# SBUF pools that wait per tile, output blocks with their own part tiles, and layer-1 modulation in parts over the whole FFN

## The chip, the cores and the metric

The kernel runs on one core of one Trainium2 chip. The metric is the device time of one execution in microseconds (us), median of several runs. Engines are named as in the profile: PE is TensorE (PEld its weight loads), DVE is VectorE, ACT is ScalarE, POOL is GpSimd, SP is SyncE, whose queue issues every DMA.

## The reference

Two blocks in a row. The first block has two layers over 512 tokens: stream 0 is the 256 context tokens, stream 1 the 256 latent tokens, D = 1024. A conditioning vector per stream gives, for each layer, six modulation rows of 1024 (shift, scale and gate of the mixer, the same of the FFN):

```
mods = silu(c) @ mod_w[l] + mod_b[l]          # rows 0..5
x = x + row2 * mixer(rmsnorm(x) * (1 + row1) + row0)
x = x + row5 * conv_ffn(rmsnorm(x) * (1 + row4) + row3)
```

Layer 0's mixer is gated linear attention and an mLSTM side by side, their outputs concatenated and multiplied by `even_w_out`; layer 1's is a state-space scan. `conv_ffn` is up-projection (1024 to 2 x 2816), a depthwise 3 x 3 convolution, silu gate, down-projection (2816 to 1024). In layer 1 only stream 1's output is needed past the mixer. The second block is one hybrid attention layer over the 256 latent tokens.

## The kernel before, in words

All activations lie features-first: 128 partitions by (8 feature chunks, 512 tokens). Each float32 weight block is loaded into a tile `st` (1 MB, 2048 columns), rounded to float16 `whi` on ACT, and the rest `st - whi` is written as bfloat16 `wlo` on DVE, or on POOL where `eng=self.G` is given (`get_w`, L318). A product takes three bfloat16/float16 passes: hi by hi, hi by lo, lo by hi (`proj_fm`, L328). `st` comes from `wst` (three buffers), the parts from `wsp` (three), unless a call names other pools (`pool`, `parts`).

Modulation row `r` of layer `l` is computed by `mod_steps` (L495), a generator of four steps per row. Each step loads 1 MB of `mod_w`. A *whole* step multiplies float32 by float32 (`cs`, 8 matmuls of 256 columns); a step *in parts* first splits the weights and multiplies by `c3`, the vector in three bfloat16 terms side by side (16 matmuls). One PSUM tile gathers the four steps, then ACT and two small matmuls make the row. `mod_first` does rows 0 and 1 of layer 0 at the start.

The stages around the change:

- `layer0_mixer` (L540): gated linear attention, then the mLSTM over four heads (`close`, L914, normalizes and writes a finished head). Their pools `gp`, `ev`, `mp` close. `xT`, the residual stream, is loaded. The tail: `whole_c` (L487) builds `cs` anew, rows 2, 3 and 4 follow as whole steps, then the four blocks of `even_o`. Blocks 0 and 1 read the attention half of the mixer's output (`h[0..3]`), blocks 2 and 3 the mLSTM half. Block 0 runs over all 512 tokens; blocks 1 to 3 per stream. `add_residual` (L533) adds the gated result to `xT`. After stream 0 comes its norm (`norm_stream`, L529).
- `ffn(0)` (L971): stream 1's norm, with two blocks of up weights begun on stream 0. 22 up blocks follow, each with convolution (`conv`, L990: ACT, then 18 DVE operations), gate (ACT, POOL) and split. After each of the first 16 blocks one modulation step is taken, after each later one two: row 5 of layer 0 and rows 0 and 1 of layer 1 in parts, rows 2 to 5 of layer 1 whole, from the pool `mp` with one buffer. Then eight down blocks of two halves (`down`, L1038), the last two per stream, with layer 1's norm of stream 0 between.
- `layer1_mixer` (L1067), `ffn(1)`, `block2` (L1421).

The order within each engine's queue is made ahead of time by Tile's scheduler (`schedule_with_timeline_sim`, L1918): among the instructions that are ready in a simulated timeline, the first in program order goes next. A later stage's work can thus come long before its place in the program, if its tiles and buffers are free; on the chip each queue then runs in that order.

A pool opened on bytes of closed pools waits: by default (`"pool"`) every tile of it waits for all users of all those closed pools; with `reuse_waits="tile"` each tile waits only for the users of the earlier tiles on its own bytes. Before, PSUM pools and the weight pools `wst`, `wsp`, `stage`, `nx`, `fw` have the latter; the others have the default.

Of the kernel before, what the change touches and what calls it, by code (L numbers as in the profile page):

```python
# [10 lines left out]
F32 = mybir.dt.float32  # L11
# [5 lines left out]
ALU = mybir.AluOpType  # L17
# [216 lines left out]
BOTH = ((0, 0, 256), (1, 256, 512))  # L234
# [14 lines left out]
class Program:  # L249
# [14 lines left out]
    def pool(self, name, bufs=1, space=None, stack=None, **kw):  # L264
        if space is not None:
            kw["space"], kw["reuse_waits"] = space, "tile"
        return (stack or self.ctx).enter_context(self.tc.tile_pool(name=name, bufs=bufs, **kw))

    def weight_sets(self, n):

        if self.w_stack is not None:
            self.w_stack.close()
        self.w_stack = self.ctx.enter_context(ExitStack())
        self.wst, self.wsp = [self.pool(t, n, None, self.w_stack, side="right", reuse_waits="tile") for t in ("wst", "wsp")]

# [127 lines left out]
    def start(self, c0):  # L403
# [9 lines left out]
        cv = ep("cv").rearrange("p (k s) -> p k s", s=2)  # L413
        self.cs = c0.tile([128, 8, 32], F32, name="cs")
        self.G.memset(self.cs, 0.0)
# [70 lines left out]

    def whole_c(self, pool):  # L487

        self.cs = pool.tile([128, 8, 32], F32, name="cs")
        self.G.memset(self.cs, 0.0)  # L490
        cs = self.cs[:, :, 0:2]
        self.tt(cs, self.c3[:, :, 2:4], self.c3[:, :, 4:6], ALU.add)
        self.tt(cs, cs, self.c3[:, :, 0:2], ALU.add)

    def mod_steps(self, l, r, tag="mm", eng=None, pool=None, parts=None, whole=False):  # L495
# [44 lines left out]
    def layer0_mixer(self):  # L540
        h, I = self.h, self.I
# [20 lines left out]
        with ExitStack() as tail:  # L562
            self.whole_c(self.pool("c0", 1, None, tail))
            for r in (2, 3, 4):
                for _ in self.mod_steps(0, r, whole=True):
                    pass
            w = self.get_w(I["even_o"][0], 4, 512)
            for c in range(4):
                ps = self.mm("eo")
                self.proj_fm(ps, w, c * 128, 128, h, 0, 512, nk=4)  # L570
                self.add_residual(ps, 0, 2, c, BOTH)

            w = [self.get_w(I["even_o"][b], 4, 512) for b in range(1, 4)]
            for s in range(2):
                for b in range(1, 4):
                    for c2 in range(2):
                        ps = self.mm("eo")
                        for c in range(2):
                            self.proj_fm(ps[:, c * 256:c * 256 + 256], w[b - 1], (2 * c2 + c) * 128, 128, h,
                                         256 * s, 256 * s + 256, nk=4, h0=4 * (b // 2))  # L580
                        for c in range(2):
                            self.add_residual(ps[:, c * 256:], 0, 2, 4 * (b % 2) + 2 * c2 + c, ((s, 0, 256),), 256 * s)
                if s == 0:
                    self.norm_stream(0, 1, 0, "ml")
        self.dbg("xmid0", self.xT)

# [384 lines left out]
    def ffn(self, l, streams):  # L971
# [6 lines left out]
        if both:  # L978

            self.norm_stream(l, 1, 1)  # L980
            first = []
            for i in range(2):
                w = self.get_w(I["w_up"][l, i], 8, 256, self.G)
                first.append((w, [self.mm("up") for _ in range(2)]))
                for c in range(2):
                    self.proj_fm(first[i][1][c][:, :256], w, c * 128, 128, h, 0, 256)
# [18 lines left out]
        with ExitStack() as ph:  # L1005
            fp = self.pool("fp", 1, None, ph)
            f2 = self.pool("f2", 3, None, ph)
            stage = self.pool("stage", 1 if both else 3, None, ph, reuse_waits="tile")
            fcw = fp.tile([128, 44, 9], F32, name="fcw")
            self.nc.sync.dma_start(fcw, I["fcw"][l].rearrange("p (c j) -> p c j", c=44))  # L1010
            hid = self.pair(fp, "hid", [128, 22, n])
            if both:
                mp = self.pool("mp", 1, None, ph)
                self.whole_c(mp)
                mods = chain(chain.from_iterable(self.mod_steps(*m, eng=self.G, pool=mp, parts=mp) for m in ((0, 5), (1, 0), (1, 1))),
                             chain.from_iterable(self.mod_steps(1, r, pool=mp, whole=True) for r in (2, 3, 4, 5)))
            for i in range(22):
                begun = both and i < 2
                if begun:
# [14 lines left out]
                self.split(hid[0][:, i], hid[1][:, i], sg[:, :n], eng=self.G)  # L1034
                for _ in range(l == 0 and (1 if i < 16 else 2)):
                    next(mods, None)

# [11 lines left out]
            for k in range(6 if both else 8):  # L1049
                self.add_residual(down(k, [weights(k, j) for j in range(2)], 0, n), l, 5, k, streams, t0)  # L1050
                if not both:
                    self.before_norm(k)
# [339 lines left out]
    def ahead(self):  # L1392

        self.nx_stack = self.ctx.enter_context(ExitStack())
        self.nx = self.pool("nx", 6, None, self.nx_stack, side="right", reuse_waits="tile")
        self.first_mg = []
# [24 lines left out]
    def block2(self):  # L1421
# [19 lines left out]
        self.weight_sets(2)  # L1441
        fw = self.pool("fw", 2, None, self.w_stack, side="right", reuse_waits="tile")

# [499 lines left out]
```

## Time and profile before

| | us |
|---|---|
| three runs | 1723.3, 1730.93, 1726.06 |
| median | 1726.06 |
| the profiled execution | 1721.83 |
| its span, first to last instruction | 1720.0 |
| granted TensorE clock over the span | 0.959 of full speed |

Busy time is the time in which an engine's instructions run. In the rows, "idle before" is the time that the engine stood still ahead of an instruction, and behind it stands what ended that. Instructions of a helper such as `tt` (L294), `stt` (L303), `act` (L306) or `proj_fm` (L332) all have the helper's line, so tile names tell them apart. Granted clock 1.0 is 2.4 GHz, half of it 1.2.

### The profile page before, as it was taken

The numbers are of one execution on the slowest core, as the hardware profiler recorded it, in microseconds if no ns is written. First come the engines' busy times: TensorE is split into PE (matmuls) and PEld (weight loads), VectorE is DVE, ScalarE is ACT, GpSimd is POOL, SyncE is SP. The second block draws the span as 40 slices with busy tenths as digits, with TensorE's granted clock in tenths as the row PEclk, the third lists the DMA queues.
The fourth block names the chain that finished last, engine by engine and source line by source line (L and its number), as shares of the span: only waits on it lengthen the run. The fifth ranks groups of instructions, "written<-read, shape, count | busy, mean of one in ns | idle before, by whom it ended". The sixth has DMA issues, their size and how long they took to land.

```text
span 1720.0 us, 31609 instructions
## 1 busy us (share of the span) xinstructions
PE 1592.1 (93%) x12912; PEld 1094.0 (64%) x12978; DVE 1190.9 (69%) x2604; ACT 824.0 (48%) x1354; POOL 489.6 (28%) x267
## 2 busy tenths in 40 slices
PE   6999999869999979999889898879999999999998
PEld 3566865556444434476556565658887787777877
DVE  5888746688777753346876767779987796366734
ACT  4746524336554422224653635446656454466542
POOL 0000000036997521001100101039964321342150
PEclk8999999889999979999999898989999999999999
DMA  9222127423555544232322222236446253243551
GB/s 378 97 83 75 52 91 272 158 98 109 187 196 189 178 172 138 94 97 86 109 74 98 74 99 74 99 128 217 170 152 219 104 188 123 92 167 129 219 174 50
DMA packets 37730, 236.77 MB, mean 138 GB/s; under 512 B 4304, under 2 KB 5072, under 8 KB 14672
## 3 DMA queue, kind: packets, MB, share of 16 engines
q1 hardware_dynamic: 37584, 234.74, 38.9%
q8 instruction: 102, 1.67, 0.4%
q14 instruction: 44, 0.36, 0.1%
HBM read 233.68 MB, written 1.05 MB: 136 GB/s over the span
## 4 chain that ended last, share of the span: by engine, by line
PE 75%; DVE 11%; issue 4%; ACT 3%; DMA 3%; POOL 2%; SPq 0%; ACTq 0%; DVEq 0%; POOLq 0%
PE up L332 17%; PE dn L332 8%; PE sx L332 5%; PE fm L332 4%; PE mg L332 3%; PE sz L332 3%; PE br L332 2%; PE so L332 2%; PE mod L509 2%; DVE wlo L294 2%; ACT whi L306 2%; POOL wlo L294 2%; PE mqk L332 2%; PE eo L332 2%; PE tm L339 1%
## 5 line engine op out<-in xcount | busy, mean ns | idle before, releaser
L332 PEld LDWEIGHTS <-whi 128*128 128x128 f16 (+2 forms) x5240 | 515.8, 100 | 266.0 <-issue 45.9
L294 POOL TENSOR_TENSOR wlo<-st,whi 128x2048 bf16<-128x2048 f32 (+2 forms) x102 | 358.6, 3520 | 648.2 <-ACT whi L306 597.9
L306 ACT ACTIVATE whi<-st 128x2048 f16<-128x2048 f32 (+3 forms) x206 | 343.5, 1673 | 303.8 <-issue 49.8
L303 DVE SCALAR_TENSOR_TENSOR u<-up,fcw,u 128x189 f32<-128x189 f32 (+3 forms) x792 | 303.7, 432 | 71.9 <-ACT u L306 61.1
L332 PEld LDWEIGHTS <-wlo 128*128 128x128 bf16 (+2 forms) x2620 | 260.7, 100 | 129.8 <-issue 14.5
L294 DVE TENSOR_TENSOR wlo<-st,whi 128x2048 bf16<-128x2048 f32 (+3 forms) x104 | 223.6, 2152 | 103.0 <-ACT whi L306 102.0
L332 PE MATMUL up<-hh,whi 128*128 128x256 f16 (+1 forms) x736 | 237.2, 325 | 2.1 <-ACT hh L306 1.8
L332 PE MATMUL up<-hh,wlo 128*128 128x256 f16 (+1 forms) x736 | 236.3, 323 | 1.9 <-issue 0.8
L332 PE MATMUL up<-hl,whi 128*128 128x256 bf16 (+1 forms) x710 | 225.9, 320 | 2.7 <-DVE hl L303 2.7
L332 PE MATMUL dn<-hidh,wlo 128*128 128x256 f16 (+1 forms) x396 | 121.4, 308 | 2.2 <-DVE wlo L294 1.7
L332 PE MATMUL dn<-hidh,whi 128*128 128x256 f16 (+1 forms) x396 | 121.3, 308 | 0.9 <-ACT whi L306 0.7
L332 PE MATMUL dn<-hidl,whi 128*128 128x256 bf16 (+1 forms) x388 | 118.5, 307 | 0.0
L490 POOL MEMSET cs<- 128x256 f32 x2 | 0.6, 312 | 288.7 <-PE yT L835 190.9
L306 ACT ACTIVATE u<-up,ppt,fcw 128x512 f32<-128x512 f32 (+1 forms) x88 | 57.9, 659 | 50.8 <-PE up L332 50.7
L332 PE MATMUL fm<-hh,wlo 128*128 128x256 f16 x288 | 78.6, 273 | 1.5 <-DVE wlo L294 1.5
L332 PE MATMUL fm<-hh,whi 128*128 128x256 f16 x288 | 78.5, 273 | 0.5 <-DVE xc L303 0.5
L332 PE MATMUL fm<-hl,whi 128*128 128x256 bf16 x288 | 78.5, 273 | 0.0
L332 PE MATMUL mg<-hh,wlo 128*128 128x256 f16 x256 | 70.9, 277 | 4.0 <-POOL wlo L294 4.0
L332 PE MATMUL mg<-hh,whi 128*128 128x256 f16 x256 | 70.6, 277 | 0.9 <-ACT mgt L306 0.9
L332 PE MATMUL mg<-hl,whi 128*128 128x256 bf16 x256 | 70.9, 277 | 0.0
L298 POOL TENSOR_SCALAR E<-E,rs 128x128 f32<-128x128 f32 (+1 forms) x48 | 37.1, 787 | 105.2 <-DVE rs L1617 47.9
L339 PEld LDWEIGHTS <-hh 128*128 128x128 f16 x640 | 61.0, 98 | 8.4 <-issue 1.1
(542 smaller groups left out, 3143.1 us busy)
## 6 DMA issues: line engine op xcount, KB each, us to landing
st<-in_w_up_dram SPq DMA_DIRECT2D x44, 1024.0 KB, 4.8
st<-in_mod_w_dram SPq DMA_DIRECT2D x40, 1024.0 KB, 4.8
st<-in_w_dram SPq DMA_DIRECT2D x25, 1024.0 KB, 4.8
st<-in_w_dn_dram SPq DMA_DIRECT2D x32, 704.0 KB, 4.1
st<-in_ssd_w_dram SPq DMA_DIRECT2D x20, 1024.0 KB, 4.8
st<-in_w_m_dram SPq DMA_DIRECT2D x32, 512.0 KB, 4.2
st<-in_even_w_dram SPq DMA_DIRECT2D x14, 1024.0 KB, 5.5
st<-in_mod_a_dram SPq DMA_DIRECT2D x8, 1024.0 KB, 16.8
```

The costliest lines, as they stand in the source:

```text
L294: (eng or self.V).tensor_tensor(o, a, b, op=op)
L298: (eng or self.V).tensor_scalar(o, a, s1, None, op0=op0)
L303: self.V.scalar_tensor_tensor(o, a, s, b, op0=op0, op1=op1)
L306: self.S.activation(o, i, func, **kw)
L332: self.T.matmul(ps, w[a][:, k, c0:c0 + cw], h[b][:, h0 + k, t0:t1], start=first and k == 0 and i == 0, stop=last and k == nk - 1 and i == 2)
L339: self.T.matmul(ps, h[b][:, k, t0:t0 + 128], w[a][:, k, c0:c0 + cw], start=k == 0 and i == 0, stop=k == nk - 1 and i == 2)
L490: self.G.memset(self.cs, 0.0)
L509: T.matmul(ps[32 * j:32 * j + 32, :256], c[:, 2 * b + k], w[:, k, 256 * j:256 * j + 256], start=b == k == i == 0, stop=b == 3 and k == 1 a ...
```

## The change

All SBUF pools get per-tile waits. `cs` is kept from the start in the constants' pool, and `whole_c` goes. In the mixer's tail the four `even_o` blocks get their parts from a pool `tw` with four buffers; blocks 0 and 1 (the attention half) run over all 512 tokens, then blocks 2 and 3 per stream; row 5 of layer 0 is done there, whole, with `tw`'s `st` tiles. In `ffn(0)` three up blocks instead of two are begun on stream 0, and all six rows of layer 1 are done in parts: one step after every second up block (11 in all), then three after each of the first down blocks.

```diff
@@ -263,15 +263,15 @@
 
     def pool(self, name, bufs=1, space=None, stack=None, **kw):
         if space is not None:
-            kw["space"], kw["reuse_waits"] = space, "tile"
-        return (stack or self.ctx).enter_context(self.tc.tile_pool(name=name, bufs=bufs, **kw))
+            kw["space"] = space
+        return (stack or self.ctx).enter_context(self.tc.tile_pool(name=name, bufs=bufs, reuse_waits="tile", **kw))
 
     def weight_sets(self, n):
 
         if self.w_stack is not None:
             self.w_stack.close()
         self.w_stack = self.ctx.enter_context(ExitStack())
-        self.wst, self.wsp = [self.pool(t, n, None, self.w_stack, side="right", reuse_waits="tile") for t in ("wst", "wsp")]
+        self.wst, self.wsp = [self.pool(t, n, None, self.w_stack, side="right") for t in ("wst", "wsp")]
 
     def set_psum(self, **tags):
 
@@ -411,7 +411,7 @@
         self.modb = ep("modb").rearrange("p (l r k) -> p l r k", l=2, r=6)
         self.ng = [ep(n).rearrange("p (l k) -> p l k", l=2) for n in ("nmix", "nffn")]
         cv = ep("cv").rearrange("p (k s) -> p k s", s=2)
-        self.cs = c0.tile([128, 8, 32], F32, name="cs")
+        self.cs = cst.tile([128, 8, 32], F32, name="cs")
         self.G.memset(self.cs, 0.0)
         self.ones = cst.tile([128, 128], F32, name="ones")
         self.G.memset(self.ones, 1.0)
@@ -483,14 +483,6 @@
             g = self.ng[0][:, 0, 2 * b:2 * b + 2]
             self.stt(modA[:, 0, :, 2 * b:2 * b + 2], modc[:, r, :, 2 * b:2 * b + 2], 1.0, bc(g, 1, 2),
                      ALU.add, ALU.mult)
-
-    def whole_c(self, pool):
-
-        self.cs = pool.tile([128, 8, 32], F32, name="cs")
-        self.G.memset(self.cs, 0.0)
-        cs = self.cs[:, :, 0:2]
-        self.tt(cs, self.c3[:, :, 2:4], self.c3[:, :, 4:6], ALU.add)
-        self.tt(cs, cs, self.c3[:, :, 0:2], ALU.add)
 
     def mod_steps(self, l, r, tag="mm", eng=None, pool=None, parts=None, whole=False):
 
@@ -560,28 +552,31 @@
         self.xT = self.res2.tile([128, 8, 512], F32, name="xT")
         self.nc.sync.dma_start(self.xT, I["xT"].rearrange("p (k t) -> p k t", k=8))
         with ExitStack() as tail:
-            self.whole_c(self.pool("c0", 1, None, tail))
+            tw = self.pool("tw", 4, None, tail)
             for r in (2, 3, 4):
                 for _ in self.mod_steps(0, r, whole=True):
                     pass
-            w = self.get_w(I["even_o"][0], 4, 512)
-            for c in range(4):
-                ps = self.mm("eo")
-                self.proj_fm(ps, w, c * 128, 128, h, 0, 512, nk=4)
-                self.add_residual(ps, 0, 2, c, BOTH)
-
-            w = [self.get_w(I["even_o"][b], 4, 512) for b in range(1, 4)]
+            w = [self.get_w(I["even_o"][b], 4, 512, parts=tw) for b in range(4)]
+
+            for b in range(2):
+                for c in range(4):
+                    ps = self.mm("eo")
+                    self.proj_fm(ps, w[b], c * 128, 128, h, 0, 512, nk=4)
+                    self.add_residual(ps, 0, 2, 4 * b + c, BOTH)
+
             for s in range(2):
-                for b in range(1, 4):
+                for b in range(2):
                     for c2 in range(2):
                         ps = self.mm("eo")
                         for c in range(2):
-                            self.proj_fm(ps[:, c * 256:c * 256 + 256], w[b - 1], (2 * c2 + c) * 128, 128, h,
-                                         256 * s, 256 * s + 256, nk=4, h0=4 * (b // 2))
+                            self.proj_fm(ps[:, c * 256:c * 256 + 256], w[2 + b], (2 * c2 + c) * 128, 128, h,
+                                         256 * s, 256 * s + 256, nk=4, h0=4)
                         for c in range(2):
-                            self.add_residual(ps[:, c * 256:], 0, 2, 4 * (b % 2) + 2 * c2 + c, ((s, 0, 256),), 256 * s)
+                            self.add_residual(ps[:, c * 256:], 0, 2, 4 * b + 2 * c2 + c, ((s, 0, 256),), 256 * s)
                 if s == 0:
                     self.norm_stream(0, 1, 0, "ml")
+            for _ in self.mod_steps(0, 5, pool=tw, whole=True):
+                pass
         self.dbg("xmid0", self.xT)
 
     def conv3(self, u, ps, w, b, streams=((0, 256), (256, 512))):
@@ -979,7 +974,7 @@
 
             self.norm_stream(l, 1, 1)
             first = []
-            for i in range(2):
+            for i in range(3):
                 w = self.get_w(I["w_up"][l, i], 8, 256, self.G)
                 first.append((w, [self.mm("up") for _ in range(2)]))
                 for c in range(2):
@@ -1005,17 +1000,15 @@
         with ExitStack() as ph:
             fp = self.pool("fp", 1, None, ph)
             f2 = self.pool("f2", 3, None, ph)
-            stage = self.pool("stage", 1 if both else 3, None, ph, reuse_waits="tile")
+            stage = self.pool("stage", 1 if both else 3, None, ph)
             fcw = fp.tile([128, 44, 9], F32, name="fcw")
             self.nc.sync.dma_start(fcw, I["fcw"][l].rearrange("p (c j) -> p c j", c=44))
             hid = self.pair(fp, "hid", [128, 22, n])
             if both:
                 mp = self.pool("mp", 1, None, ph)
-                self.whole_c(mp)
-                mods = chain(chain.from_iterable(self.mod_steps(*m, eng=self.G, pool=mp, parts=mp) for m in ((0, 5), (1, 0), (1, 1))),
-                             chain.from_iterable(self.mod_steps(1, r, pool=mp, whole=True) for r in (2, 3, 4, 5)))
+                mods = chain.from_iterable(self.mod_steps(1, r, eng=self.G, pool=mp, parts=mp) for r in range(6))
             for i in range(22):
-                begun = both and i < 2
+                begun = both and i < 3
                 if begun:
                     w, pss = first[i]
                 else:
@@ -1032,8 +1025,8 @@
                 self.act(sg[:, :n], us[1][:, :n], AF.Silu)
                 self.tt(sg[:, :n], sg[:, :n], us[0][:, :n], ALU.mult, eng=self.G)
                 self.split(hid[0][:, i], hid[1][:, i], sg[:, :n], eng=self.G)
-                for _ in range(l == 0 and (1 if i < 16 else 2)):
-                    next(mods, None)
+                if both and i % 2:
+                    next(mods)
 
             def down(k, ws, a, b):
                 ps = self.mm("dn")
@@ -1048,6 +1041,8 @@
                 self.ahead()
             for k in range(6 if both else 8):
                 self.add_residual(down(k, [weights(k, j) for j in range(2)], 0, n), l, 5, k, streams, t0)
+                for _ in range(3 if both else 0):
+                    next(mods, None)
                 if not both:
                     self.before_norm(k)
                     if k >= 4 and k < 4 + 3:
```

The two other hunks only drop `reuse_waits="tile"` from pools that now get it from `pool`.

## Rows read from the trace of the kernel before

**Rows 1.** Page, part 1: busy time (share of the span) and instructions of the engines.

```profile
...
PE 1592.1 (93%) x12912; PEld 1094.0 (64%) x12978; DVE 1190.9 (69%) x2604; ACT 824.0 (48%) x1354; POOL 489.6 (28%) x267
...
```

**Rows 2.** Table by stretch: length, busy time of each engine, granted clock, DMA share, GB/s.

```profile
...
301.00:382.00 81.00, 56.77 (x399) 42.95 (x398) 62.17 (x138) 27.41 (x46) 16.68 (x5) 0.87 0.35 124
382.00:596.00 214.00, 212.70 (x1288) 104.23 (x1312) 162.76 (x414) 107.90 (x117) 158.09 (x63) 0.99 0.50 169
596.00:665.00 69.00, 56.62 (x327) 24.33 (x327) 38.34 (x86) 16.74 (x21) 13.78 (x9) 0.85 0.49 175
665.00:790.00 125.00, 123.51 (x750) 71.94 (x757) 49.77 (x91) 32.91 (x43) 3.19 (x2) 1.00 0.32 105
...
```

**Rows 3.** Timeline of TensorE, 305 to 385 us: start, duration, what; idle before and its releaser.

```profile
...
309.96 0.61 PE L332 MATMUL eo<-hh,whi 128*128 128x512 f16 x1 [2.39 <-DVE xT L303]
...
333.74 1.08 PE L918 MATMUL yT<-ept,hm 128*128 128x128 f32 x4 [3.20 <-DVE hm L294]
...
381.41 0.99 PE L367 MATMUL ssq<-ones,sq 128*128 128x1 f32 x4 [11.63 <-DVE sq L294]
...
```

**Rows 4.** Timeline of GpSimd, 336 to 400 us (columns as in rows 3).

```profile
...
341.84 4.07 POOL L294 TENSOR_TENSOR wlo<-st,whi 128x2048 bf16<-128x2048 f32 x1 [6.50 <-ACT whi L306]
...
376.09 4.16 POOL L294 TENSOR_TENSOR wlo<-st,whi 128x2048 bf16<-128x2048 f32 x1 [5.30 <-ACT whi L306]
```

**Rows 5.** VectorE by form, 336 to 398 us: count, busy us, mean ns; an undisturbed sum.

```profile
...
L294 DVE TENSOR_TENSOR sq<-sq,s 128x256 f32<-128x256 f32 x14 | 12.7, 908 | 3.1 <-ACT s L306 2.6
L303 DVE SCALAR_TENSOR_TENSOR hl<-nt,modc,hh 128x256 bf16<-128x256 f32 x16 | 10.7, 699 | 0.9 <-ACT hh L306 0.9
L303 DVE SCALAR_TENSOR_TENSOR xT<-eo,modc,xT 128x256 f32<-128x256 f32 x20 | 8.8, 477 | 5.5 <-PE eo L332 5.5
...
L303 DVE SCALAR_TENSOR_TENSOR r<-rt,r 128x2 f32<-128x2 f32 x6 | 4.8, 800 | 0.2
...
L303 DVE SCALAR_TENSOR_TENSOR rt<-rt,v 128x2 f32<-128x2 f32 x6 | 1.0, 161 | 0.2
...
364.87 0.42 DVE L294 TENSOR_TENSOR sq<-sq,s 128x256 f32<-128x256 f32 x1 [0.54 <-ACT s L306]
...
```

**Rows 6.** Timeline of VectorE: last `hl` of the mixer, first `nt` of stream 1.

```profile
...
335.68 0.74 DVE L303 SCALAR_TENSOR_TENSOR hl<-yT,ppt,hh 128x512 bf16<-128x512 f32 x1
...
388.01 0.87 DVE L303 SCALAR_TENSOR_TENSOR nt<-xT,modA,rbc 128x256 f32<-128x256 f32 x2 [1.80 <-PE rbc L375]
```

**Rows 7.** Chain of waits and timeline of TensorE, 590 to 665 us.

```profile
...
596.48 7.49 DMA st<-in_mod_w_dram
...
621.98 1.00 PE mod L509 x16
...
604.01 1.94 PE L509 MATMUL mod<-st,cs 128*32 128x256 f32 x16 [3.17 <-DMA st<-in_mod_w_dram]
...
610.97 1.93 PE L509 MATMUL mod<-st,cs 128*32 128x256 f32 x16 [3.49 <-DVE u L303]
...
644.03 1.94 PE L509 MATMUL mod<-st,cs 128*32 128x256 f32 x16 [3.22 <-DVE u L303]
...
```

**Rows 8.** Chain of waits: matmuls in a row, 512 columns (dn) and 256 (up).

```profile
...
718.92 10.96 PE dn L332 x50
...
1146.80 78.37 PE up L332 x703
...
```

**Rows 9.** Timelines of SyncE's DMA queue and GpSimd: one modulation step in the first FFN.

```profile
...
410.00 0.33 SPq L315 DMA_DIRECT2D st<-in_mod_w_dram  x1
...
421.04 0.33 SPq L315 DMA_DIRECT2D st<-in_mod_w_dram  x1
...
416.93 4.08 POOL L294 TENSOR_TENSOR wlo<-st,whi 128x2048 bf16<-128x2048 f32 x1 [1.68 <-ACT whi L306]
...
```

**Rows 10.** VectorE groups: split of down weights, 665 to 790 us; the FFN convolution (page, part 5).

```profile
...
L294 DVE TENSOR_TENSOR wlo<-st,whi 128x1408 bf16<-128x1408 f32 x13 | 21.0, 1625 | 29.7 <-ACT whi L306 29.7
...
L303 DVE SCALAR_TENSOR_TENSOR u<-up,fcw,u 128x189 f32<-128x189 f32 (+3 forms) x792 | 303.7, 432 | 71.9 <-ACT u L306 61.1
...
```

More of the change, by code (lines that the diff above doesn't have):

```diff
@@ L1394, in ahead @@
         self.nx_stack = self.ctx.enter_context(ExitStack())
-        self.nx = self.pool("nx", 6, None, self.nx_stack, side="right", reuse_waits="tile")
+        self.nx = self.pool("nx", 6, None, self.nx_stack, side="right")
         self.first_mg = []
@@ L1441, in block2 @@
         self.weight_sets(2)
-        fw = self.pool("fw", 2, None, self.w_stack, side="right", reuse_waits="tile")
+        fw = self.pool("fw", 2, None, self.w_stack, side="right")
         def fm(b, eng=None):
```

## The prediction

> **What bounds the kernel now.** I read the page first: TensorE is busy 1592 of 1720 us [rows 1], so only places where it idles or runs slowly can give anything back. The table by stretch then shows where these lie around the change [rows 2]. From 382 to 596 us (the first FFN's up-projections) TensorE is busy 212.7 of 214 us, from 665 to 790 us (the down-projections) 123.5 of 125: nothing to win there. From 301 to 382 us, the end of the layer-0 mixer and the norm ahead of the FFN, it is busy 56.8 of 81 us at a granted clock of 0.87; from 596 to 665 us, the end of the up loop, 56.6 of 69 at 0.85. The idle time is 24.2 and 12.4 us.
>
> The timeline of TensorE names the gaps of the first stretch [rows 3]: 2.4 us for a residual, 3.2 us for the last mLSTM head's norm, and 11.6 us in which `ssq` of stream 1 waits for VectorE's sum of squares. VectorE is the engine behind that: from 336 to 398 us its operations are stretched [rows 5]. The 14 sums of squares average 0.91 us, where an undisturbed one takes 0.42; the 16 `hl` average 0.70, where the residual update `xT` of the same size takes 0.48; six two-element `r` updates average 0.80, where `rt` of the same size takes 0.16. That is 14 x 0.49 + 16 x 0.22 + 6 x 0.64 = 14 us of stretching. GpSimd runs just four operations there, the 4.1 us splits `wlo` (the first and the last of the four in [rows 4]); 14 us is 3.5 for each, one VectorE operation held during nearly a whole split. So the splits of the first FFN weights (three) and of the first modulation step (one) sit in VectorE's critical chain. They come that late because `w_up`'s parts need a slot of `wsp`, and all three slots hold `even_o` blocks 1 to 3 until stream 1 is projected.
>
> In the second stretch the chain of waits and the timeline show modulation steps at the head of TensorE's queue [rows 7]: one waits for a weight transfer that takes 7.49 us, the next two for a PSUM bank that a late convolution still reads: gaps of 3.2, 3.5 and 3.2 us, and the step after each gap takes twice as long (1.93 us for 16 matmuls against 1.00). From i = 16 on, two whole-precision steps fall in one iteration.
>
> **The sum, part by part** (against the profiled execution, 1721.8 us; it is 4.2 us below the median of 1726.06).
>
> *Tail, weights split early.* `even_o` gets its parts from the pool `tw`, so `wsp` is free and the three `w_up` splits can run while the last mLSTM head is still computed. From the head's last `hl` (335.68) to the first `nt` of stream 1 (388.01) the chain is 52.3 us [rows 6]. Three of four held operations leave it: -10.5. Block 1's stream-1 residuals (4 x 0.48 [rows 5]) also go ahead of it: -1.9. That leaves 39.9 us on VectorE. TensorE's work in it: two `even_o` blocks in both streams, 192 matmuls of 256 columns at 0.111 us (78.37/703 [rows 8]) = 21.4; three `up` blocks for stream 0, 144 x 0.111 = 16.0; modulation row 5, 4 steps at 0.5 (16 matmuls, two whole steps, in 1.00 [rows 7]; a step in parts is taken the same) = 2.0; the two norms' small matmuls, 0.99 for four [rows 3], about 2: 41.4 us. I take 41.4. Gain 10.9, and the third `up` block for stream 0 (48 x 0.111 = 5.3) is done inside it: 16.2. Against this, the three splits now meet VectorE in the last head, whose norm is a chain of small operations: each can hold it up to 3.5 us, 10.5 in all; TensorE has 5.3 us more to do there (block 1, stream 1) beside the 5.6 us of gaps it has [rows 3]. I charge 4. Net **-12**; ends: -4 (all three splits on the chain) and -18 (none).
>
> *Tail, row 5 moved.* Four DMA issues, 32 whole-precision matmuls, one row of ACT and two of VectorE come ahead of the FFN, past `w_up` in SP's queue. By the tile sizes in the code, `tw` (64 KB a partition, behind the 16 KB of `xT`) reaches into the bytes of `yf`, which the last head still reads; if SP's queue has these loads before `w_up`'s, the early splits are lost, which is the -4 end above. The fourth `wlo` of `even_o` may wait there too, at most its own 2.4 us (1.63 us for 1408 columns [rows 10], scaled to 2048). Inside the charge of 4.
>
> *`whole_c` and `cs`.* A memset and two small adds go: 0, they lie beside other work.
>
> *End of the up loop.* Eleven steps instead of 28, one in two iterations, none whole: the three gaps (9.9 us), the two doubled steps (2 x 0.93) and the slow matmuls after them go: **-13**; ends -8 (a gap for a PSUM bank stays) and -16. TensorE's own work there falls by 17 x 0.5 = 8.5, but 13 steps come to the down loop (+6.5) and 4 to the tail (counted): 0 in sum.
>
> *Down loop.* A step's cycle through its single buffers is load at 410.00, GpSimd's split from 416.93 on, next load at 421.04: 11.0 us [rows 9]. Three steps per block ask for one in 4.8 us (a block is 66 matmuls at 0.219 = 14.5 us [rows 8]). The scheduler orders TensorE's queue by a simulated time, so the steps fall behind rather than stop it: 13 steps need about 12 x 11.0 + 5 = 137 us, and the eight blocks with the steps' own matmuls take 8 x 14.5 + 6.5 = 122. They overrun by some 15 us into layer 1's norm, with one or two splits that hold VectorE (3.5 us each) and a PSUM bank that layer 1's eight want. ACT and VectorE are idle enough inside the loop (VectorE busy 50 of 125 us [rows 2]). Cost **+3**; ends 0 (the overrun is covered by stream 0's projections) and +15 (TensorE waits through it).
>
> What the row shows of the conflict: sums and `hl`, which take two operands from SBUF, are held; the convolution's `u`, with one operand in PSUM, averages 0.43 us over all 792 although GpSimd is busy 158 of 214 us beside it [rows 2, 10]. The Trainium skill (SBUF — State Buffer, section "SBUF: two separate sides") calls the pair of ports that VectorE and GpSimd share an exclusive lock for a whole instruction, taken by a VectorE operation with two SBUF inputs against a GpSimd operation that reads SBUF; the trace agrees. It speaks against this change, which has 24 modulation splits on GpSimd instead of 12: if each of the 12 new ones held the critical chain for 3.5 us, that alone would be +42 us and the sum positive. By the rows they fall where VectorE has slack, so I keep +3.
>
> *Other pools' waits.* At the borders of layer 1, the second FFN and block 2 the first tiles of the new pools lie on bytes used to the end of the old phase (`fcw` on `ys`): 0, ends -5 and +3 from a changed order.
>
> Sum: -12 - 13 + 3 = **-22 us**: 1699.8 by the profiled execution, **1704** by the median.
>
> **Rivals.**
> *A, the early splits don't help.* SP's queue, or the last head's chain, takes back the tail's gain. For: the head is a chain of small VectorE operations, and `tw` reaches into `yf`. Against: TensorE has work to fill. -4 or less there: -22 + 8 to 12, about **1714**.
> *B, more moves forward.* With per-tile waits the scheduler may start FFN and layer-1 loads still earlier. For: the output projection `eo` runs at 309.96, 26 us ahead of the head's end that stands before it in the program [rows 3, 6]. Against: little idle time is left elsewhere. -18, -16, 0, -5: **1687**.
> *C, slower: the steps in the down loop hold layer 1.* If a step's cycle is over about 15 us (SP's queue holds `w_dn` loads in front, ACT and VectorE their splits), 13 steps take 195 us, 70 over the loop; the last row's bank and VectorE then stop layer 1's norm, whose stream-0 projections cover some 25. Price 45, minus 25: **1746**. It decides from a cycle of about 13 us. Against: 11.0 us was measured beside heavier traffic (169 GB/s from 382 to 596, 105 in the down loop [rows 2]).
> *D, the order is shuffled to no effect*: **1724**.
>
> **Numbers.** Forecast 0.52, A 0.15, B 0.14, C 0.10, D 0.09. A measurement of this kernel tells about 0.5%, 8.6 us, from no change. Faster: the forecast, B, and most of A, 0.77; same: the rest of A and D, 0.13; slower: C, 0.10. The range goes from B to just short of D: 1685 to 1722.
>
> **What would show it.** Right: no GpSimd `wlo` between the last head and the first `nt` of stream 1 but the modulation step's; the wait at `ssq` under 4 us; three `up` blocks before stream 1; TensorE busy over 98% at the end of the up loop; modulation steps 11 us apart in the down loop, the last one in layer 1's norm. Wrong: `w_up`'s splits still after the last head (A), or TensorE idle over 10 us at layer 1's start (C).

## The result, and the profile after

| | before | after |
|---|---|---|
| median of eight runs, us | 1723.84 (1721.70 to 1730.93) | 1739.3 (1733.65 to 1743.93) |
| the profiled execution, its span, us | 1721.83, 1720.0 | 1741.26, 1739.4 |
| granted TensorE clock over the span | 0.959 | 0.953 |

The ratio is 1.008, interval 1.006 to 1.0101: slower, by 15 us, which is under 1% but clear of the interval. 1704 was forecast, and the range ended at 1722.

TensorE's busy time grew by 6 us, as the page's first part shows for after against [rows 1]: 13 of the 19 us between the spans are idle time.

```profile
PE 1598.1 (92%) x12978; PEld 1101.4 (63%) x12978; DVE 1190.8 (68%) x2600; ACT 845.1 (49%) x1366; POOL 538.7 (31%) x277
```

To see where, I cut both traces at the first `up` matmul, the first `dn` matmul and the last `dn` matmul of the first FFN. The table by stretch of before (columns as in [rows 2]), up loop and down loop:

```profile
382.25:658.28 276.03, 262.40 (x1569) 125.43 (x1596) 195.78 (x488) 122.44 (x137) 171.87 (x72) 0.96 0.50 170
658.28:775.84 117.56, 117.14 (x695) 66.23 (x701) 44.77 (x68) 31.34 (x37) 3.19 (x2) 1.00 0.33 109
```

The same of after:

```profile
367.53:606.53 239.00, 237.20 (x1386) 121.37 (x1386) 191.57 (x486) 119.37 (x133) 166.87 (x70) 1.00 0.38 129
606.53:788.57 182.04, 137.99 (x893) 73.36 (x890) 64.28 (x74) 56.23 (x54) 57.83 (x17) 0.85 0.37 132
```

| stage | before | after | difference |
|---|---|---|---|
| up to the first `up` matmul | 382.25 | 367.53 | -14.7 |
| up loop | 276.03 | 239.00 | -37.0 |
| down loop | 117.56 | 182.04 | +64.5 |
| from there to the end of the span | 944.2 | 950.8 | +6.7 |

After is 51.7 us ahead when the down loop begins and 12.7 behind when it ends. In that loop TensorE is idle for 182.04 - 137.99 = 44.0 us, against 0.4, and its granted clock is 0.85. The steps' own matmuls take 15.4 us of it, against 2.7 (the last two steps of before fell in this loop too), and the other matmuls take 8.1 more than before, at the lower clock. The code behind the loop is the same; in the kernels below it takes 942 to 955 us, 944 and 955 in two executions of one of them, so I read nothing into 6.7.

**The down loop.** The chain of waits of after, 628 to 672 us:

```profile
628.88 4.72 DMA st<-in_mod_w_dram
...
641.68 6.09 DMA st<-in_mod_w_dram
647.88 1.92 ACT whi L306
649.86 4.07 POOL wlo L294
653.95 4.70 DMA st<-in_mod_w_dram
658.75 1.92 ACT whi L306
660.74 4.06 POOL wlo L294
664.82 4.99 DMA st<-in_mod_w_dram
669.89 1.92 ACT whi L306
671.86 0.41 PE mod L501 x4
```

Load, ACT, GpSimd and the next load follow each other, 11 us a turn (653.95 - 641.68 = 12.3, 664.82 - 653.95 = 10.9): just the cycle of [rows 9], and now it is the chain that sets the end. TensorE's timeline of after shows who stands still for it:

```profile
649.84 0.41 PE L501 MATMUL mod<-whi,c 128*32 128x256 f16 x4 [7.06 <-ACT whi L306]
653.97 0.41 PE L501 MATMUL mod<-wlo,c 128*32 128x256 bf16 x4 [3.73 <-POOL wlo L294]
660.71 0.41 PE L501 MATMUL mod<-whi,c 128*32 128x256 f16 x4 [5.91 <-ACT whi L306]
664.84 0.41 PE L501 MATMUL mod<-wlo,c 128*32 128x256 bf16 x4 [3.73 <-POOL wlo L294]
671.86 0.41 PE L501 MATMUL mod<-whi,c 128*32 128x256 f16 x4 [4.67 <-ACT whi L306]
```

All gaps but one of 0.55 us stand ahead of a `mod` matmul, and from 642.3 to 672.2 us no `dn` matmul starts at all: three steps begin one right behind the other in the queue, and the block after them waits until the first matmuls of the third have their weights. That block could have run. VectorE's timeline of after has the last split of down weights ahead of it, and the next one comes only at 684.68:

```profile
643.56 1.62 DVE L294 TENSOR_TENSOR wlo<-st,whi 128x1408 bf16<-128x1408 f32 x1 [0.32 <-ACT whi L306]
```

So its weights had been there since 645.2, and it stood 27 us behind the steps. The same comes once more with two steps from 705.6 to 722.6 us (gaps of 2.92, 3.73 and 7.29 us; some 1.9 of the last come from SyncE's queue, which issues the step's load at 714.50, behind one for layer 1, though GpSimd is done with the buffer at 712.6). From there on 47 or more `dn` matmuls lie from the start of one step to that of the next, and no gap over 0.8 us is left.

**The tail.** Timeline of TensorE of after, against [rows 3]:

```profile
314.33 0.61 PE L332 MATMUL eo<-hh,whi 128*128 128x512 f16 x1 [4.46 <-ACT whi L306]
...
361.64 3.66 PE L501 MATMUL mod<-st,cs 128*32 128x256 f32 x64
366.01 0.61 PE L508 MATMUL mod<-ept,mrow 128*128 128x8 f32 x4 [0.72 <-ACT mrow L306]
366.75 0.58 PE L367 MATMUL ssq<-ones,sq 128*128 128x1 f32 x4
367.53 0.27 PE L332 MATMUL up<-hh,whi 128*128 128x256 f16 x1 [0.20 <-DVE modc L294]
```

The gap of 11.63 ahead of stream 1's `ssq` is gone. A new one of 4.46 stands ahead of the output projection. VectorE of after by form, 328 to 390 us, against [rows 5]:

```profile
L294 DVE TENSOR_TENSOR sq<-sq,s 128x256 f32<-128x256 f32 x14 | 9.3, 662 | 1.7 <-ACT s L306 1.0
L303 DVE SCALAR_TENSOR_TENSOR hl<-nt,modc,hh 128x256 bf16<-128x256 f32 x16 | 7.3, 480 | 0.7 <-ACT hh L306 0.7
...
L303 DVE SCALAR_TENSOR_TENSOR r<-rt,r 128x2 f32<-128x2 f32 x6 | 1.0, 159 | 0.2
```

`hl` and `r` are undisturbed now, and the excess of the sums of squares over 0.42 us has halved. Why it is not gone: SyncE's queue of after has row 5's loads ahead of the up weights, and so GpSimd's four splits come at the end of the last head and behind it. Timelines of SyncE and GpSimd of after:

```profile
311.89 2.22 SPq L315 DMA_DIRECT2D st<-in_mod_w_dram  x4
316.62 0.33 SPq L315 DMA_DIRECT2D st<-in_even_o_dram  x1
318.90 2.60 SPq L315 DMA_DIRECT2D st<-in_w_up_dram  x2
...
331.92 16.17 POOL L294 TENSOR_TENSOR wlo<-st,whi 128x2048 bf16<-128x2048 f32 x4 [293.56 <-ACT whi L306]
```

And VectorE's timeline of after, against [rows 6]:

```profile
331.58 0.75 DVE L303 SCALAR_TENSOR_TENSOR hl<-yT,ppt,hh 128x512 bf16<-128x512 f32 x1
...
344.59 4.84 DVE L294 TENSOR_TENSOR sq<-sq,s 128x256 f32<-128x256 f32 x3
...
374.34 0.87 DVE L303 SCALAR_TENSOR_TENSOR nt<-xT,modA,rbc 128x256 f32<-128x256 f32 x2 [0.85 <-PE rbc L375]
```

Three sums take 4.84 us, where three undisturbed ones take 1.3: one operation held, 3.5 us, not four. During the other splits VectorE ran residual updates, which read PSUM and kept their 0.48 us. The chain from the last `hl` to stream 1's first `nt` is 42.8 us, against 52.3.

### The profile page after: what moved, and what is told of

The parts are those of the page before. It is cut to its first block, busy times and chain, and to the rows that moved or that the text cites. A ratio compares the mean times of both kernels' runs of the same rounds, so it can differ in the third digit from the quotient of the medians.

```text
span 1739.4 us, 31681 instructions
## 1 busy us (share of the span) xinstructions
PE 1598.1 (92%) x12978; PEld 1101.4 (63%) x12978; DVE 1190.8 (68%) x2600; ACT 845.1 (49%) x1366; POOL 538.7 (31%) x277
## 4 chain that ended last, share of the span: by engine, by line
PE 73%; DVE 10%; ACT 5%; DMA 5%; issue 3%; POOL 2%; ACTq 0%; SPq 0%; DVEq 0%; POOLq 0%
PE up L332 19%; PE dn L332 6%; PE sx L332 5%; PE fm L332 4%; PE mg L332 3%; ACT whi L306 3%; DVE wlo L294 3%; PE sz L332 2%; PE tm L339 2%; PE so L332 2%; PE br L332 2%; DMA st<-in_mod_w_dram 2%; POOL wlo L294 2%; DMA st<-in_w_m_dram 2%; PE mqk L332 2%
## 5 line engine op out<-in xcount | busy, mean ns | idle before, releaser
L294 POOL TENSOR_TENSOR wlo<-st,whi 128x2048 bf16<-128x2048 f32 (+2 forms) x114 | 407.8, 3581 | 952.2 <-ACT whi L306 892.1
L306 ACT ACTIVATE whi<-st 128x2048 f16<-128x2048 f32 (+3 forms) x218 | 365.4, 1685 | 339.0 <-DMA st<-in_mod_w_dram 55.8
L332 PEld LDWEIGHTS <-wlo 128*128 128x128 bf16 (+2 forms) x2620 | 259.6, 99 | 131.1 <-issue 14.3
L294 DVE TENSOR_TENSOR wlo<-st,whi 128x2048 bf16<-128x2048 f32 (+3 forms) x104 | 242.9, 2338 | 134.9 <-ACT whi L306 133.8
L303 DVE SCALAR_TENSOR_TENSOR u<-up,fcw,u 128x189 f32<-128x189 f32 (+3 forms) x792 | 298.1, 430 | 46.0 <-ACT u L306 37.0
L332 PE MATMUL up<-hl,whi 128*128 128x256 bf16 (+1 forms) x752 | 237.3, 317 | 3.3 <-DVE hl L303 3.3
L332 PE MATMUL dn<-hidh,whi 128*128 128x256 f16 (+1 forms) x396 | 125.0, 317 | 2.0 <-ACT whi L306 1.7
L332 PE MATMUL dn<-hidl,whi 128*128 128x256 bf16 (+1 forms) x396 | 125.3, 318 | 0.0
L332 PE MATMUL sx<-hl,whi 128*128 128x512 bf16 (+1 forms) x160 | 53.8, 337 | 0.0
```

The costliest lines, as they stand in the source:

```text
L294: (eng or self.V).tensor_tensor(o, a, b, op=op)
L303: self.V.scalar_tensor_tensor(o, a, s, b, op0=op0, op1=op1)
L306: self.S.activation(o, i, func, **kw)
L332: self.T.matmul(ps, w[a][:, k, c0:c0 + cw], h[b][:, h0 + k, t0:t1], start=first and k == 0 and i == 0, stop=last and k == nk - 1 and i == 2)
```

## The experiments

Theory 1, formed on the traces above: the cycle of a step (11 us, one buffer for `st` and one for the parts) is longer than the distance of the steps in TensorE's queue; TensorE works its queue in order and stops. In the program three steps follow each block of 66 `dn` matmuls of 0.219 us, one step in 4.8 us. In the queue of after, by its trace, 350 `dn` matmuls lie between the start of the first step and that of the last of the 13: 29, or 6.4 us, from one step to the next on the mean, and none at three places. The rivals: the new steps cost through GpSimd or VectorE wherever they lie; the per-tile waits or the tail lose time. Each experiment shared its runs of the kernel before (median 1721.6 to 1722.4 us in all three groups); ratios are to it.

**st2**: after, with two buffers for the steps' loads and still one for their parts.

```
-  ...mod_steps(1, r, eng=self.G, pool=mp, parts=mp)...
+  ms = self.pool("ms", 2, None, ph)
+  ...mod_steps(1, r, eng=self.G, pool=ms, parts=mp)...
```

> The changed kernel with two load buffers for the modulation steps in the first FFN (parts still one each). Theory 1, the cycle of a step: in the down loop TensorE's queue holds a step every 5 us or so of down matmuls, but a step's load can only start when the split before it has read the one load buffer, so a step takes 11.0 us and TensorE stands in front of each. With two buffers the load runs beside the split before it, the cycle is 1.9 + 4.1 = 6.0 us, and most of the 42 us of gaps go: about 1700 us, gaps in front of modulation matmuls under 12 us. Theory 2, SyncE's queue: the loads come late because they stand behind down-weight loads that wait for their buffers; then a second buffer changes little, 1730 or more. Theory 3, GpSimd's splits hold VectorE's splits of the down weights: same number of splits, so 1735 or more.

Measured: 1704.94 us, 0.9909 [0.9885, 0.9932]. The down loop takes 152.0 us, of which 20.1 idle. TensorE's timeline of this kernel:

```profile
642.93 0.40 PE L501 MATMUL mod<-whi,c 128*32 128x256 f16 x4 [2.61 <-ACT whi L306]
647.06 0.40 PE L501 MATMUL mod<-wlo,c 128*32 128x256 bf16 x4 [3.73 <-POOL wlo L294]
649.74 0.40 PE L501 MATMUL mod<-whi,c 128*32 128x256 f16 x4 [1.84 <-ACT whi L306]
653.87 0.41 PE L501 MATMUL mod<-wlo,c 128*32 128x256 bf16 x4 [3.73 <-POOL wlo L294]
```

With the load off the cycle a turn is 6.8 us (653.87 - 647.06). Where steps stand one right behind the other TensorE still stops for it, so nearly half of the idle time stays; theory 1 had expected under 12 us. One buffer more turns the change from slower to faster.

**spread**: after, with 17 steps in the up loop and 7 in the down loop.

```
-  if both and i % 2:
+  if both and i % 4 != 3:
...
-  for _ in range(3 if both else 0):
+  for _ in range((2 if k == 0 else 1) if both else 0):
```

> The changed kernel with the modulation steps moved out of the down loop: one step after three of every four up blocks (17), two after the first down block and one after each of the next five (7). Theory 1: a step every 11 us or more is what the cycle gives, so the gaps in the down loop fall from 42 to under 8 us, and the gains of the tail and of the end of the up loop stay: about 1690. Theory 2: seven loads instead of thirteen behind down-weight loads, about half of the loss goes: 1715. Theory 3: seven splits instead of thirteen beside VectorE's, 1715.

Measured: 1693.87 us, 0.983 [0.9792, 0.9868]. The table by stretch of its down loop:

```profile
616.65:738.43 121.78, 121.78 (x791) 67.55 (x788) 59.30 (x70) 43.61 (x45) 32.53 (x10) 1.00 0.44 148
```

No idle time is left, at a clock of 1.00; the up loop grows by 7 us (246.1). The same 24 steps, the same GpSimd splits: their places alone were the loss.

**onlymods**: before, with only the new schedule of the steps (row 5 in front, 28 steps in parts, tail unchanged).

```
-  mods = chain(... (0, 5), (1, 0), (1, 1) in parts, (1, 2) to (1, 5) whole)
+  mods = chain.from_iterable(self.mod_steps(*m, eng=self.G, pool=mp, parts=mp) for m in ((0, 5),) + tuple((1, r) for r in range(6)))
...
-  for _ in range(l == 0 and (1 if i < 16 else 2)):
+  for _ in range(both and (2 if i in (0, 5, 10, 15) else i % 2)):
...
+  for _ in range(3 if both else 0):
+      next(mods, None)
```

> The kernel before with only the modulation schedule changed: row 5 of layer 0 and all six rows of layer 1 in parts, 17 of the 28 steps in the up loop and up to 11 in the down loop, three per block; the tail, the pools' waits and two up blocks as before. Theory 1: the down loop stands as in the changed kernel, 30 to 45 us of gaps, less the 11 at the end of the up loop that go: 1745 to 1760. If the loss needs the per-tile waits as well, 1715 to 1725.

Measured: 1741.2 us, 1.0113 [1.0089, 1.0138], a little under theory 1's range. The up loop falls to 244.9 us, the down loop rises to 166.0, of which 33.8 idle (166.0 - 132.2). The table by stretch of its down loop:

```profile
624.80:790.80 166.00, 132.19 (x858) 71.50 (x854) 57.73 (x73) 52.28 (x51) 49.48 (x14) 0.88 0.38 132
```

The slowdown comes with this part alone.

**oldmods**: after, with the old schedule of the steps (row 5 stays in the tail).

```
-  mods = chain.from_iterable(... in parts ... for r in range(6))
+  mods = chain(... r in (0, 1) in parts, r in (2, 3, 4, 5) whole)
...
-  if both and i % 2:
+  for _ in range(l == 0 and (1 if i < 16 else 2)):
...
-  for _ in range(3 if both else 0):
-      next(mods, None)
```

> The changed kernel with the modulation schedule of before: rows 0 and 1 of layer 1 in parts, rows 2 to 5 whole, one step per up block, two from block 16 on, none in the down loop. It prices the tail with its output blocks, early splits and the third up block alone. All theories of the down loop: its 42 us of gaps are gone; the gap at the end of the up loop may come back in part, since row 5 is no longer in it and the steps end four earlier. 1697 to 1706 if the tail is worth some 17 to 25 us; over 1715 if the tail is worth little.

Measured: 1712.85 us, 0.9946 [0.9929, 0.9963], between the two cases expected. The first `up` matmul runs at 365.83, near that of after (367.53); the loops take 278.4 and 115.0 us, much as before. The table by stretch of its down loop:

```profile
644.24:759.21 114.97, 114.97 (x666) 65.13 (x665) 45.04 (x69) 30.88 (x36) 3.65 (x3) 1.00 0.30 99
```

So the tail is worth some 9 us of the end time, and the two parts are of opposite sign.

**e5_waits**: before, with only the per-tile waits.

```
-            kw["space"], kw["reuse_waits"] = space, "tile"
+            kw["space"] = space
+        kw["reuse_waits"] = "tile"
```

> The kernel before with one edit, the per-tile waits in all SBUF pools. Theory 1 (the loss of the change comes from the steps in the down loop, its gains from the tail's parts in their own pool and from the up loop): the waits alone are worth little, ratio to before 0.996 to 1.002 (1716 to 1727 us), and the 11.6 us gap ahead of ssq stays, since the up weights' parts still want the slots that even_o holds. Theory 2 (the waits make the gain in the tail): 1705 to 1712 us, and that gap is under 5 us. Theory 3 (the waits shuffle the queues for the worse and are part of the loss): over 1730 us.

Measured: 1719.73 us, 0.9994 [0.9969, 1.0019]; the gap ahead of `ssq` is 11.62 us. In the time that is nothing, as theory 1 has it. Ahead of that gap the waits do move something: the chain from the last `hl` to stream 1's first `nt` takes 48.3 us instead of 52.3, with the sums of squares at 0.70 us instead of 0.91.

**f1_spread_poolwaits**: spread, with the default waits back in the SBUF pools that had them.

```
+        if space is not None or name in ("wst", "wsp", "stage", "nx", "fw"):
+            kw["reuse_waits"] = "tile"
```

> The spread version (17 steps in the up loop, 7 in the down loop; 1694 us) with the old waits put back in the SBUF pools that had them before the change. Theory 1 (the waits are worth little): 1690 to 1700 us. Theory 2 (without them the tail's pool tw, whose bytes the last mLSTM head still reads, waits for the whole mixer, so that the early products and splits are lost): 1705 us or more, and TensorE's first up matmul of the first FFN at 378 us or later instead of 370.6.

Measured: 1688.05 us, 0.9821 [0.9779, 0.9864], first `up` matmul at 366.68, and the time a little under theory 1's range. The new waits are no condition of the tail's gain either.

**f2_spread_two**: spread, with `range(2)` and `i < 2` for the begun up blocks.

> The spread version with two up blocks instead of three begun ahead of stream 1's norm. If the third block is cover for the norm (48 matmuls of 0.111 us): 5 us slower than spread, 1696 to 1702 us, and the idle time ahead of stream 1's norm grows by as much. If VectorE's chain is short enough by now that two blocks cover it: 1692 to 1696 us, no difference.

Measured: 1682.06 us, 0.9771 [0.9745, 0.9798], below both expectations, which leaned on the 1694 of spread from another group. So both went once more, side by side.

**g2_two_again**, **g3_three_again**: the same two kernels.

> The spread version with two begun up blocks once more, beside the one with three on the same chip, since the two came from different jobs: 1679 to 1686 us. If the third block is worth nothing or less: equal to three or up to 8 us faster; if it covers: 3 to 6 us slower than three.

> The spread version (three begun up blocks) once more, beside the one with two. From its earlier runs 1686 to 1699 us; if the distance of 12 us between the two was a matter of the chip, within 4 us of the one with two.

Measured: two blocks 1685.05 us, 0.9781 [0.9756, 0.9807]; three 1682.36, 0.977 [0.9744, 0.9796]. Two blocks are 2.7 us slower, within the noise of both and just short of the 3 to 6 of cover. The traces show no cover: from the first `up` to the first `dn` matmul the kernels take 245.8 and 246.1 us. So the third block, for which I counted 5.3 us, covers nothing that two leave open and that these runs could measure. The kernel with three gave 1693.9 and 1682.4 us in two groups, so distances under 1% between groups say nothing here.

**e6_whole**: after, with layer 1's rows 3 to 5 as whole steps, which need neither ACT nor GpSimd.

```
-  mods = chain.from_iterable(... in parts ... for r in range(6))
+  mods = chain(... r in (0, 1, 2) in parts, r in (3, 4, 5) whole)
```

> The changed kernel with layer 1's rows 3 to 5 as whole steps (no split on ACT and GpSimd), their places in the loops kept: 11 steps in the up loop, 13 in the down loop. Theory 1 (the loss is the cycle of a step in parts, load, ACT, GpSimd, 11 us, against places some 5 us apart in TensorE's queue): a whole step's cycle is its load and its matmuls, 5 to 7 us, so the idle time ahead of the steps in the down loop falls from 42 us to under 15, and each of 12 whole steps costs 0.5 us more of TensorE: 1705 to 1715 us. Theory 2 (it is the load of 1 MB through SP's queue that is late, not the split): the gaps stay above 25 us and the time above 1725.

Measured: 1707.33 us, 0.9922 [0.9894, 0.9951]. The down loop takes 149.9 us, 14.3 of them idle, and what ends the gaps is now the load. TensorE's timeline of this kernel:

```profile
645.02 1.70 PE L501 MATMUL mod<-st,cs 128*32 128x256 f32 x16 [4.82 <-DMA st<-in_mod_w_dram]
...
651.71 1.93 PE L501 MATMUL mod<-st,cs 128*32 128x256 f32 x16 [3.42 <-DMA st<-in_mod_w_dram]
```

A shorter cycle at the same places in the program leaves a third of the idle time: theory 1 again, from the side of the split instead of the load.

**g1_onlyspread**: onlymods, with the places `i != 21` in the up loop (21 steps) and `2 if k == 0 else 1` in the down loop (7).

> The kernel before with only the modulation steps changed: rows 5 of layer 0 and 0 to 5 of layer 1 in parts, 21 steps in the up loop (one per block, 48 matmuls of 0.219 us = 10.5 us apart), 7 in the down loop (14.5 us apart); tail, pools and two begun up blocks as before. Theory 1 (a place closer than the cycle of 11.0 us costs, a wider one doesn't): the down loop is free of idle time, dn from 117 to 121 us; in the up loop each step is at most 0.5 us late, so no gap of over 1 us; the 11.6 us gap ahead of ssq stays. 1721 less the idle time and slow clock at the end of the old up loop (12 + 6) less some 8 us of whole steps: 1694 to 1704 us. Theory 2 (the new rows in parts cost of themselves, through GpSimd and ACT, wherever they lie): over 1715 us.

Measured: 1700.28 us, 0.987 [0.9844, 0.9896]; down loop 121.8 us, the 11.63 gap as before, no gap over 1 us in the up loop. Steps in parts, well placed, take 22 us off the kernel before by themselves.

**f3_row5_in_ffn**: spread, with row 5 of layer 0 back in the FFN, in parts, and the places of g1_onlyspread.

```
-            for _ in self.mod_steps(0, 5, pool=tw, whole=True):
-                pass
...
-  mods = ... (1, r, ...) for r in range(6))
+  mods = ... (*m, ...) for m in ((0, 5),) + tuple((1, r) for r in range(6)))
...
-  if both and i % 4 != 3:
+  if both and i != 21:
```

> The spread version with row 5 of layer 0 taken out of the mixer's tail and put back into the FFN in parts (21 steps in the up loop, 7 in the down loop, as in the kernel before with only spread steps). If row 5's four loads in SP's queue hold the fourth even_o block and the up weights, as the trace of the changed kernel has it: the 4 us gap ahead of eo goes, and the up weights' splits run before the last head's end; four whole steps (4 x 0.9 us) become steps in parts (4 x 0.6): 3 to 8 us less than spread. If the four more steps in the up loop come too close (10.5 us for a cycle of 11.0): the same as spread or up to 8 us more. Against the kernel before with only spread steps, the difference is what the tail's new order is worth: 10 to 20 us less.

Measured: 1702.17 us, 0.9871 [0.9841, 0.9901]: 20 us more than g3_three_again beside it and level with g1_onlyspread. Every expectation missed. TensorE's timeline and, as its last row, the table by stretch of this kernel:

```profile
365.72 0.98 PE L367 MATMUL ssq<-ones,sq 128*128 128x1 f32 x4 [5.04 <-DVE sq L294]
...
426.78 0.29 PE L501 MATMUL mod<-wlo,c 128*32 128x256 bf16 x4 [2.44 <-POOL wlo L294]
...
433.65 0.40 PE L501 MATMUL mod<-whi,c 128*32 128x256 f16 x4 [5.26 <-ACT whi L306]
...
400.00:440.00 40.00, 31.44 (x178) 14.47 (x180) 28.17 (x74) 22.17 (x24) 39.44 (x17) 0.87 0.59 195
```

Two things are to be seen. With row 5's loads away the four splits do run at the last head (GpSimd from 325.40 to 341.95), no sum of squares is held any more, and yet stream 1's `ssq` waits 5.04 us for VectorE: the chain is that long by itself, and in after row 5's 3.66 us of matmuls filled the wait. Then the up loop, which takes 262.4 us against 246.1: near its start GpSimd is busy all the time, here 39.44 of 40 us and in g3_three_again 40.00. With a step at three blocks in four TensorE (39.68 of the 40 us busy there) stands at none; with one at every block it is busy 31.44. The two gaps shown are the only ones over 1 us in this loop, though the steps go on at every block. Why they come there, and why g1_onlyspread, with the same places, has none, I did not settle; its loop starts 15 us later.

## Why the prediction was wrong

**The step that failed** is the down loop's: "The scheduler orders TensorE's queue by a simulated time, so the steps fall behind rather than stop it". The cycle was right (11.0 forecast, 10.9 and 12.3 measured) and so was the demand, one step in 4.8 us. But the order that came out lets the steps fall behind only in part: it has 29 `dn` matmuls from one to the next on the mean, where a cycle of 11 us would need 50, and none at three places. A step late on the chip stops everything behind it. So the steps did start 11.6 us apart on the mean, from 620.2 to 758.9 us, as forecast, but because TensorE stood and waited for them. I took +3 with ends 0 and +15 for what measured 43.6 us of idle time and 8.1 of slower matmuls. That the queue can stop stood in my own rows: all three gaps of [rows 7] are TensorE standing at a step. st2 and e6_whole shorten the cycle, spread widens the distance, and of 44.0 us of idle time 20.1, 14.3 and 0 are left.

**The up loop was mis-sized the other way.** By stage I had -13 for gaps and slow matmuls and -8.5 for 17 steps; 37.0 went. Idle time fell from 13.6 to 1.8 us, about as forecast; the matmuls of the steps fell from 30.7 to 7.8 us, not by 8.5. The row of 16 matmuls in 1.00 us [rows 7] is one whole step, not two: the trace lists 16 for the 8 of the code, as row 5's four steps show in after (x64). A whole step takes 0.92 us there, a step in parts 0.62 (11 in 6.8 us in after's up loop). All steps together cost 30.7 + 2.7 us before and 7.8 + 15.4 + 4.3 after, so that my "0 in sum" over the stages is off by 6.

**The tail was right in size, in part by luck**: -12 forecast, -14.7 at the first `up` matmul, and some 9 us at the end (oldmods). The chain of 41.4 us measured 42.8, but its terms were others. `eo` filled 30 us of it, not 21.4, since most of block 1 still ran behind the last `hl`; row 5 took 5.0, not 2.0; and fewer than 40 of the 144 matmuls of the three `up` blocks, for which I had 16.0, came ahead of the first `nt`. My charge of 4 for splits inside the last head was not taken: the splits came after it, and in f3_row5_in_ffn, where they run beside it, it is no longer either (18.8 us from the third `hl` to the last, 19.9 in g3_three_again). Rival A's cause and sign came true, with `mod_w` ahead of `w_up` in SyncE's queue and the splits behind the head, and its price did not: it cost one held operation.

**Rival C** was next to the measured time (1746), and so to the sign, but by another way: it let the steps hold layer 1's norm and "decides from a cycle of about 13 us". They held TensorE inside the loop, and what decided was a cycle longer than the distance in the queue, 6.4 us on the mean.

**The ports.** VectorE's held operations were told rightly: three of four went, and the one left is 3.5 us long. The Trainium skill (SBUF — State Buffer, section "SBUF: two separate sides") calls that pair of ports an exclusive lock, and by it I worked out +42 us for 12 more splits. That the idle time in the down loop came out at 43.6 is a coincidence: the gaps end with ACT and GpSimd, not with VectorE, and spread has as many splits and no idle time. Beside GpSimd's splits VectorE's splits of down weights do take longer (4.33 us at 636.91, for 1.62 at 643.56); one of them, at 709.73, stands on the chain ahead of the late load at 714.50, so up to 1.9 of the 43.6 us can be the ports'.

**The rest.** The waits of the other pools: 0 forecast, 0 measured in the time, alone and in the good version. The third begun block: 5.3 counted, nothing found.

## What to carry to other kernels

For work strewn into an in-order matmul queue, put the cycle of its feed (load, split on one engine, split on the next, buffer free again) beside the distance between its places in the queue: if the cycle is longer over a run of places, the queue stops for about the difference, however idle the other engines look. (One close place alone can pass: spread has two starts 8.8 us apart behind two that are 14.2 apart, and no stop.) A second buffer or a shorter cycle mended half of it or more here, wider places all of it; the same steps gave 1739 us three to a block and 1682 to 1694 with six of them moved into the longer loop. Before costing a moved item by a row of the trace, count how many records one item makes.

## What the hardware showed that I had not expected

A float32 step, 8 matmuls in the code, is listed as 16 and takes 1.00 us in a busy stretch [rows 7]; a step in parts, 16 matmuls in the code, took 0.6. And a stop costs more than its own length: in after, from 622 to 722 us, with TensorE busy 57.5 of 100 us, the granted clock averages 0.76, against 0.99 and 1.00 in the first and the last stretch of the FFN before [rows 2]. Four `mod` matmuls take 0.41 us behind those gaps and 0.29 ahead of them, and the matmuls of the loop that are not of steps 8.1 us more in all.
